# Folding the squared tiles of three norm entrances on VectorE, and moving the decay product behind the output gate, in a two-layer fp32 trunk

## The chip, the cores and the metric

The kernel runs on one core of one Trainium2 chip, in one launch. The metric is the device time in microseconds, from the first to the last instruction with what lies around them; of several runs the median is given. Five engines run their own instruction streams in program order and wait for one another by semaphores: TensorE (PE, its weight loads listed apart as PEld), VectorE (DVE), ScalarE (ACT), GpSimd (POOL) and SyncE (SP), which issues most of the DMAs.

## The reference

A trunk of two layers on x (1, 1024, 1024), all in fp32. Each layer is a token mixer and a dense SwiGLU channel mixer, each behind an RMS norm that is shifted and scaled by a conditioning vector. Layer 0's mixer is forgetting attention (FoX), layer 1's is gated linear attention (GLA).

```python
def rms_norm(x, g):
    xf = x.astype(jnp.float32)
    y = xf * lax.rsqrt(jnp.mean(xf * xf, axis=-1, keepdims=True) + EPS)
    return (y * g.astype(jnp.float32)).astype(x.dtype)

def gated_linear_attention(h, w_in, w_a2, b_a, g_o, w_out):
    proj = h @ w_in
    q, k, v, r, a_lr = jnp.split(proj, [...], axis=-1)
    log_alpha = jax.nn.log_sigmoid((a_lr @ w_a2 + b_a)) / GLA_TAU
    ...
    b = jnp.cumsum(log_alpha.reshape(B, N, CHUNK, GLA_HEADS, GLA_HK), axis=2)
    q_in = q * jnp.exp(b)
    k_in = k * jnp.exp(-b)
    A = tril(jnp.einsum('bnthk,bnshk->bnhts', q_in, k_in))
    k_dec = k * jnp.exp(b_last[:, :, None] - b)
    ...
    o = (o_intra + o_inter) * rsqrt(mean(o * o) + EPS) * g_o
    return (o * jax.nn.silu(r)) @ w_out

for i in range(DEPTH):
    h = modulate(rms_norm(x, norm1_g[i]), sh1, sc1)
    x = x + g1 * (forgetting_attention(h) if i % 2 == 0 else gated_linear_attention(h))
    h = modulate(rms_norm(x, norm2_g[i]), sh2, sc2)
    x = x + g2 * ((silu(h @ w_gate) * (h @ w_up)) @ ffn_w_out[i])
return rms_norm(x, final_g)
```

## The kernel before

Activations lie transposed: eight tiles of 128 features by 1024 tokens, worked on in two token halves of 512. Every fp32 product is three matmuls of high and low parts (lines 290, 291 and 292), so a product over 1024 features is 24 of them, of 512 columns each. FFN products go through sums and differences of sub-blocks (tiles `p_b`, with operands made from raw weights `xv_s` and `ex_s` by GpSimd at line 889 and after).

**Norm entrances.** The three entrances that matter here are the FFN of layer 0, the GLA mixer of layer 1 and the FFN of layer 1. `last_chunk` adds the last product's eight output tiles, one by one, into the residual x (line 1328). Behind each tile ScalarE squares it (line 764), and `SumSq.__call__` (line 771) adds squares pairwise, as a tree. For the second token half at these entrances (`late` = LATE1 = 7) the tree stops at four tiles, v0, v4, v6 and v7. Each of them is summed over its 128 features on TensorE, by four matmuls (`sp_b`, line 758: 128 tokens as weights, a column of ones as data), all accumulating in one PSUM bank. SUM_AT lets the first root's four go ahead, behind tile 5; the other twelve stand together later. In a profile such an fp32 matmul has two records, so sixteen matmuls show as 8 and 24. Then VectorE scales and adds epsilon (line 700), GpSimd takes the power −0.5 (line 701), and TensorE spreads the result over the partitions (`rb_b`, line 710), from where VectorE makes the normed input. The first token half is done earlier and is not touched.

**What sets the order.** Each engine's order is set ahead of time. Where the code asks for it with `issue_after`, an instruction is placed behind another in its engine's order. At the FFN entrances the work is the first products on the first token half, and the tuple GK says before which of the eight steps of the second plain tile the sums and the row broadcast stand. At the mixer `gv_first` plays that role: value products of one token tile each (`gv_b`, 24 matmuls of 272 columns), of which those for token tiles 0 to 3 need the first half only.

**The GLA mixer, head 0.** Behind the norm come the output gate's products `gr` (one per token half, 24 matmuls), the transposed low-rank gate inputs (`aps`, `a_body`), the decay product `z` (one matmul per half, line 1909), the key products `gk` and query products `gqp` (24 matmuls per half each). From z the decay is made: absolute value and minimum (1910, 1911), Exp and Ln (1918, 1919), a difference and two scans on VectorE (1923), Exp tiles (1933, 1934), which multiply gk out of PSUM (1948, 1949). `gr`, `z`, `gk` and `gqp` take turns in the three PSUM banks of the ring `pj`; a product can start when the readers of its bank are through. Weights come by DMA into a ring of three raw tiles (line 212), are cast to the high part on ScalarE (227) and subtracted to the low part in four pieces, three on GpSimd and one on VectorE (231). SP issues these loads in order, among those for the next layer vectors (`ad_s`, 427), which VectorE sums (488, 490).

Of the kernel before, what the change touches and what calls it, by code (L numbers as in the profile page):

```python
# [9 lines left out]
F32 = mybir.dt.float32  # L10
# [6 lines left out]
P = 128  # L17
# [3 lines left out]
HALF = 512  # L21
# [32 lines left out]
def trunk(ctx, tc, x, c, ada_w, ada_b, norm1_g, norm2_g, ffn_w_in, ffn_w_out,  # L54
# [54 lines left out]
    def psl(t, n=1):  # L109
        return slice(t * P, (t + n) * P)  # L110
# [576 lines left out]

    sp_ins, rb_ins, root_ins = [], [], {}
    LATE1 = 7
    SUM_AT = {5: 1, 7: 2}  # L690
    GK = (2, 6)
    SPM, RBM = (3, 4)

    def rms_cols(ss, nm, psr, n=4):

        ss.sums(psr, len(ss.roots))
        sp = ss.sp
        sp_ins.append(last_ins())
        rs = sm.tile([P, n], F32, tag="rs", name=f"rs{nm}")
        nc.vector.tensor_scalar(rs, sp, 1.0 / D, EPS, op0=ALU.mult, op1=ALU.add)  # L700
        nc.gpsimd.tensor_tensor(rs, rs, mhalf[:, 0:n], op=ALU.pow)
        root_ins.update(D=last_of("D"), G=last_of("G"))
        return rs
# [38 lines left out]
    class SumSq:  # L742


        def __init__(self, v, hf, late):
            w = slice(256 * (hf % 2), 256 * (hf % 2) + 256) if hf > 1 else slice(0, HALF)
            self.v = [v[i][:, w] for i in ((1, 3, 2, 5, 7, 6, 3, 4) if hf else range(8))]
            self.late = late
            self.n, self.sp, self.done = (2 if hf > 1 else 4), None, 0
            self.roots = {0: [self.v[0]], 8: [self.v[0]], 7: [self.v[0], self.v[4], self.v[6], self.v[7]]}[late]  # L750

        def sums(self, psr, upto):

            if self.sp is None:
                self.sp = psr([P, self.n], F32, "sp")
            for i in range(self.done, upto):
                for t in range(self.n):
                    nc.tensor.matmul(self.sp[:, t:t + 1], self.roots[i][:, psl(t)], ones, start=i == t == 0,
                                     stop=i == len(self.roots) - 1 and t == self.n - 1)
            self.done = upto  # L760

        def __call__(self, m, xk):
            v = self.v
            nc.scalar.activation(v[m], xk, AF.Square)
            if self.late == 0:
                if m:
                    nc.vector.tensor_add(v[0], v[0], v[m])
                return
            d = 1
            while m & d and m < self.late:  # L770
                (nc.gpsimd if d == 1 and m < 4 else nc.vector).tensor_add(v[m - 2 * d + 1], v[m - 2 * d + 1], v[m - d + 1])
                d *= 2

# [556 lines left out]
                if after is not None:  # L1330
                    after(m, hf)

    def last_chunk(k0, kc, hs, xs, l, j, nm, v, norm, mt=2, each=None, meanwhile=None, psr=None):


        behind = None
        for hf in (0, 2, 3) if each else (0, 1):
            sq = SumSq(v, hf, (0 if each else LATE1) if hf else 8)

            def after(m, h_, sq=sq):  # L1340
                sq(m, xs[m][:, hsl(h_)])
                if h_ == 1 and m in SUM_AT:
                    sq.sums(psr, SUM_AT[m])
                if each:
                    each(m, h_)
# [47 lines left out]
    def ffn(l, oh, xs, slots, nm, mid, norm_end, each=None):  # L1393
# [52 lines left out]
                split_t((b["B11"] + b["B21"])[k], ya[k], sh(k))  # L1446
            return gates

        last_chunk(4, 4, oh, xs, l, 2, nm, sv, norm, psr=psr)
        dump(f"xa{l}", xs)  # L1450
        sg = opr_["sg"]
        rb = rms_rows(ss1[0], f"{l}11", psr)
# [336 lines left out]
        sv = Views(slots["b"][0:4], 2, [HALF], f"se{l}").v  # L1789
        tmp = Views(slots["to"], 2, [HALF], f"te{l}")  # L1790
        last_chunk(NFH - 4, 4, hp, xs, l, 5, f"f{l}e", sv,
                   lambda hf, ss: norm_end(hf, ss, tmp), mt=1, each=each, meanwhile=meanwhile, psr=norm_banks)

    pin = None
    slots = ffn_slots(rest)
# [79 lines left out]
        nc.vector.tensor_sub(aT[32:48, cs], ps, aT[0:16, cs].bitcast(F32))  # L1875
        nc.scalar.copy(aT[64:80, cs], ps)

    def gv_first(t, wv, behind=None):

        if t % 2 == 0:  # L1880
            vt.append(vr([P, 2, 2, 256], FR, f"gvt0{t}"))
        ps = gvr([P, 272], F32, f"gv0{t}")
        with tc.issue_after(behind) if behind is not None else ExitStack():
            run(proj_tok(ps, wv, h1, t))
        nc.scalar.copy(aS[:, t], ps[:, 256:272])
        v = vt[-1]
        split(v[:, 0, t % 2], v[:, 1, t % 2], ps[:, 0:256])
# [49 lines left out]
    def head_front(h, b16, t2, ei, nmid):  # L1937
# [4 lines left out]
        for hf in range(2):  # L1942
            cs = hsl(hf)
            ps = pj([P, HALF], F32, f"gk{h}{hf}")
            run(proj(ps, wk, h1, hf))
            ada1(5.1)
            y = yv()
            nc.vector.tensor_mul(y, ps, ei[:, cs])
# [104 lines left out]
    def r_proj(h, gs, done):  # L2053
        wr_ = [None, None]
        for hf, dv in ((0, 0), (0, 1), (1, 0), (1, 1)) if h else ((0, 0), (1, 0), (0, 1), (1, 1)):
            if wr_[dv] is None:
                wr_[dv] = feed.next()
            ps = pj([P, HALF], F32, f"gr{h}{dv}{hf}")
            yield from proj(ps, wr_[dv], h1, hf)
            ada1(5.1)  # L2060
            nc.scalar.activation(gs[dv][:, hsl(hf)], ps, AF.Silu)
# [6 lines left out]
        w2_split()  # L2068
    split_after.update(marks)
    gvr = Ring(psp, list(pj.q) + list(opr.q))  # L2070
    aS = big.tile([P, 8, 16], F32, tag=kdr.q[0], name="aS")
    vt = []
    gv_first(0, wv)
    gv_first(1, wv)
    with tc.issue_after(sp_ins[-1]):
        gv_first(2, wv)
        gv_first(3, wv, rb_ins[-1])
    split_after.update((e, last_of(e)) for e in "AD")
    with behind_all():
        for f in rest_of_norm:  # L2080
# [9 lines left out]
        bt = gate_z(0, (0,))  # L2090
    for t in range(4, 8):
        gv_first(t, wv)
    while (0, 1) not in done:
        next(rg)
    a_body(1)
    b16, t2, ei, dec = gate_body(0, gate_z(0, (1,), bt))
    gtile = {}
    for h in range(4):
        dec, nmid = dec
# [102 lines left out]
```

## Time and profile before

| what | value |
|---|---|
| median of 3 runs | 2389.67 us (2388.23 to 2390.68) |
| profiled execution, its own time | 2393.87 us |
| its span, first to last instruction | 2392.2 us |
| mean granted TensorE clock | 0.991 |
| PE busy | 2362.3 us, 99% |
| DVE, ACT, POOL busy | 74%, 47%, 44% |
| longest waits of PE at the places of the change | 2.9 us (gqp), 1.3 us (gk) |

Busy shares are of the span. Rows of the timeline give start, duration, engine, line, operation, output and input tiles, shapes, a count, and in brackets how long the engine had been idle and what ended that. A row with x24 holds 24 records that followed each other, and its duration reaches from the first's start to the last's end.

### The profile page before, as it was taken

The numbers are of one execution on the slowest core, as the hardware profiler recorded it, in microseconds if no ns is written. First come the engines' busy times: TensorE is split into PE (matmuls) and PEld (weight loads), VectorE is DVE, ScalarE is ACT, GpSimd is POOL, SyncE is SP. The second block draws the span as 40 slices with busy tenths as digits, with TensorE's granted clock in tenths as the row PEclk, the third lists the DMA queues.
The fourth block names the chain that finished last, engine by engine and source line by source line (L and its number), as shares of the span: only waits on it lengthen the run. The fifth ranks groups of instructions, "written<-read, shape, count | busy, mean of one in ns | idle before, by whom it ended". The sixth has DMA issues, their size and how long they took to land.

```text
span 2392.2 us, 35827 instructions
## 1 busy us (share of the span) xinstructions
PE 2362.3 (99%) x12312; PEld 2012.5 (84%) x12312; DVE 1770.5 (74%) x2985; ACT 1128.8 (47%) x2178; POOL 1046.5 (44%) x976
## 2 busy tenths in 40 slices
PE   8999999999999999999999999999999999999998
PEld 6988888888888888888888798898888888888888
DVE  6577787886698788875798566655687877765787
ACT  6656565675443333345325555453443333345326
POOL 1334444533445566643264321212345666643262
PEclk8999999999999999999999999999999999999999
DMA  8423333342435545457655233334424544457664
GB/s 259 142 80 113 104 119 93 119 133 89 150 109 174 178 165 168 166 203 258 228 188 166 82 105 90 99 112 132 150 91 154 179 148 161 154 180 255 230 205 147
DMA packets 336366, 363.47 MB, mean 152 GB/s; under 512 B 24924, under 2 KB 278008, under 8 KB 336184
## 3 DMA queue, kind: packets, MB, share of 16 engines
q1 hardware_dynamic: 336184, 361.18, 46.3%
q8 instruction: 97, 1.59, 0.3%
q14 instruction: 85, 0.70, 0.1%
HBM read 268.22 MB, written 92.86 MB: 151 GB/s over the span
## 4 chain that ended last, share of the span: by engine, by line
PE 82%; DVE 8%; DMA 4%; ACT 2%; issue 2%; POOL 1%; SPq 1%; DVEq 0%; POOLq 0%; ACTq 0%
PE p_b L290 15%; PE p_b L292 15%; PE p_b L291 15%; PE o_b L1224 2%; PE t_b L1210 2%; PE qk_b L290 1%; PE qk_b L291 1%; PE qk_b L292 1%; PE gr_b L290 1%; PE gr_b L291 1%; PE vps_b L292 1%; PE vps_b L290 1%; PE vps_b L291 1%; PE gr_b L292 1%; PE s_b L1178 1%
## 5 line engine op out<-in xcount | busy, mean ns | idle before, releaser
L175 DVE TENSOR_TENSOR o_s<-xv_s,o_s 128x512 fp32r<-128x512 f32 (+1 forms) x376 | 326.7, 874 | 67.7 <-ACT o_s L174 67.3
L174 ACT CAST o_s<-xv_s 128x512 fp32r<-128x512 f32 (+1 forms) x376 | 216.4, 587 | 304.3 <-PE p_b L292 244.5
L291 PE MATMUL p_b<-B,o_s 128*128 128x512 f32 x608 | 237.8, 391 | 0.0
L292 PE MATMUL p_b<-B,o_s 128*128 128x512 f32 x608 | 237.2, 391 | 0.0
L290 PE MATMUL p_b<-B,o_s 128*128 128x512 f32 x608 | 236.0, 391 | 0.0
L889 POOL TENSOR_TENSOR ex_s<-xv_s,xv_s 128x512 f32<-128x512 f32 (+1 forms) x64 | 88.5, 1382 | 286.7 <-DMA xv_s<-in_ffn_w_in_dram 113.6
L1190 POOL TENSOR_SCALAR lp_s<-lp_s,st 128x128 f32<-128x128 f32 (+7 forms) x128 | 97.9, 769 | 249.5 <-DVE st L1189 235.5
L290 PE MATMUL p_b<-T,o_s 128*128 128x512 f32 x480 | 186.7, 389 | 0.0
L291 PE MATMUL p_b<-T,o_s 128*128 128x512 f32 x480 | 186.7, 389 | 0.0
L292 PE MATMUL p_b<-T,o_s 128*128 128x512 f32 x480 | 181.2, 389 | 0.0
L292 PEld LDWEIGHTS p_b<-B,o_s 128*128 128x128 f32 x608 | 114.7, 189 | 24.0
L290 PEld LDWEIGHTS p_b<-B,o_s 128*128 128x128 f32 x608 | 114.7, 189 | 23.9
L291 PEld LDWEIGHTS p_b<-B,o_s 128*128 128x128 f32 x608 | 114.7, 189 | 23.7
L1188 ACT ACTIVATE lp_s<-lp_s,st 128x128 f32<-128x128 f32 (+7 forms) x128 | 99.3, 776 | 62.3 <-DVE st L1184 61.2
L891 POOL TENSOR_TENSOR xv_s<-ex_s,xv_s 128x512 f32<-128x512 f32 (+1 forms) x64 | 87.3, 1365 | 63.1 <-DVE o_s L175 60.8
L174 ACT CAST pt_s<-t_b 128x512 fp32r<-128x512 f32 (+1 forms) x160 | 79.8, 547 | 71.9 <-PE t_b L1210 71.3
L231 POOL TENSOR_TENSOR w_l_s<-w__s,w_h_s 128x256 fp32r<-128x256 f32 x90 | 69.6, 802 | 94.2 <-ACT w_h_s L227 61.8
L175 DVE TENSOR_TENSOR pt_s<-t_b,pt_s 128x512 fp32r<-128x512 f32 (+1 forms) x160 | 96.3, 630 | 15.9 <-ACT pt_s L174 15.4
L1572 DVE TENSOR_TENSOR ex_s<-ex_s,p_b 128x512 f32<-128x512 f32 x140 | 93.6, 681 | 18.6 <-PE p_b L292 18.5
L290 PEld LDWEIGHTS p_b<-T,o_s 128*128 128x128 f32 x480 | 90.1, 188 | 18.8
L291 PEld LDWEIGHTS p_b<-T,o_s 128*128 128x128 f32 x480 | 90.1, 188 | 18.7
L292 PEld LDWEIGHTS p_b<-T,o_s 128*128 128x128 f32 x480 | 90.1, 188 | 18.6
(1967 smaller groups left out, 7408.3 us busy)
## 6 DMA issues: line engine op xcount, KB each, us to landing
xv_s<-in_ffn_w_in_dram SPq DMA_DIRECT2D x176, 256.0 KB, 3.3
hid_B<-x SPq DMA_DIRECT2D x70, 512.0 KB, 2.8
ad_s<-in_ada_w_dram SPq DMA_DIRECT2D x384, 64.0 KB, 2.4
hid_T<-x SPq DMA_DIRECT2D x36, 512.0 KB, 2.8
xv_s<-in_ffn_w_out_dram SPq DMA_DIRECT2D x96, 192.0 KB, 5.1
ada_s<-in_ada_w_dram SPq DMA_DIRECT2D x96, 128.0 KB, 2.8
xv_s<-in_ffn_w_out_dram SPq DMA_DIRECT2D x40, 256.0 KB, 2.8
T2o<-hid_T SPq DMA_DIRECT2D x18, 512.0 KB, 9.7
```

The lines of the kernel that those rows point to most:

```text
L174: nc.scalar.copy(hi, src)
L175: nc.vector.tensor_sub(lo, src, hi.bitcast(F32))
L231: (nc.gpsimd if i < 3 else nc.vector).tensor_sub(lo[:, cs], rw[:, cs], hi[:, cs].bitcast(F32))
L290: nc.tensor.matmul(ps, ah, bh, start=start, stop=False)
L291: nc.tensor.matmul(ps, ah, bl, start=False, stop=False)
L292: nc.tensor.matmul(ps, al, bh, start=False, stop=stop)
L889: nc.gpsimd.tensor_add(s1, a21, a22)
L891: nc.gpsimd.tensor_sub(a11, s1, a11)
L1188: nc.scalar.activation(lp, lp, AF.Exp, bias=mcur, scale=-1.0, accum_out=st[:, qi, 2:3])
L1190: nc.gpsimd.tensor_scalar(lp, lp, st[:, qi, 3:4], 1.0, op0=ALU.mult, op1=ALU.mult)
L1210: nc.tensor.transpose(tp[:, i, :], lps[qi][:, psl(2 * b + jj)], ident)
L1572: nc.vector.tensor_add(d, d if src is None else dest(G, src), ps)
```

## The change

Three things are changed. First, at the three entrances VectorE folds all eight squared tiles of the second token half into v0, in the order of their coming, and TensorE sums v0 alone, with four matmuls; the early part is gone. Second, the sums and the row broadcast stand one step later at the FFN entrances (GK from 2 and 6 to 3 and 7), and at the mixer within `gv_first(3)`. Third, in GLA head 0 the first `gr` product takes the bank of `atr`, the ring `pj` is turned by one, and the order on TensorE is set by hand: two steps of the second `gr`, the gate inputs' transposes, the rest of `gr`, z of the second half, and only then `gk`.

```diff
     LATE1 = 7
-    SUM_AT = {5: 1, 7: 2}
-    GK = (2, 6)
+    GK = (3, 7)
...
-        ss.sums(psr, len(ss.roots))
+        ss.sums(psr)
...
-            self.n, self.sp, self.done = (2 if hf > 1 else 4), None, 0
-            self.roots = {0: [self.v[0]], 8: [self.v[0]], 7: [self.v[0], self.v[4], self.v[6], self.v[7]]}[late]
-
-        def sums(self, psr, upto):
-
-            if self.sp is None:
-                self.sp = psr([P, self.n], F32, "sp")
-            for i in range(self.done, upto):
-                for t in range(self.n):
-                    nc.tensor.matmul(self.sp[:, t:t + 1], self.roots[i][:, psl(t)], ones, start=i == t == 0,
-                                     stop=i == len(self.roots) - 1 and t == self.n - 1)
-            self.done = upto
+            self.n = 2 if hf > 1 else 4
+            self.root = self.v[0]
+
+        def sums(self, psr):
+
+            self.sp = psr([P, self.n], F32, "sp")
+            for t in range(self.n):
+                nc.tensor.matmul(self.sp[:, t:t + 1], self.root[:, psl(t)], ones, start=t == 0, stop=t == self.n - 1)
...
+            if m > 4 and self.late == LATE1:
+                if m == 5:
+                    nc.vector.tensor_add(v[4], v[4], v[5])
+                    nc.vector.tensor_add(v[0], v[0], v[4])
+                else:
+                    nc.vector.tensor_add(v[0], v[0], v[m])
+                return
             d = 1
-            while m & d and m < self.late:
+            while m & d:
...
                 sq(m, xs[m][:, hsl(h_)])
-                if h_ == 1 and m in SUM_AT:
-                    sq.sums(psr, SUM_AT[m])
...
-    def gv_first(t, wv, behind=None):
+    def gv_first(t, wv, after=()):
...
-        with tc.issue_after(behind) if behind is not None else ExitStack():
-            run(proj_tok(ps, wv, h1, t))
+        g = proj_tok(ps, wv, h1, t)
+        for k in range(8):
+            with ExitStack() as es:
+                for k_, ins in after:
+                    if k >= k_:
+                        es.enter_context(tc.issue_after(ins))
+                next(g)
...
             ps = pj([P, HALF], F32, f"gk{h}{hf}")
-            run(proj(ps, wk, h1, hf))
+            with ExitStack() if h else tc.issue_after(z_last):
+                run(proj(ps, wk, h1, hf))
...
-            ps = pj([P, HALF], F32, f"gr{h}{dv}{hf}")
+            ps = (pj if h or hf or dv else atr)([P, HALF], F32, f"gr{h}{dv}{hf}")
...
     gvr = Ring(psp, list(pj.q) + list(opr.q))
+    pj.q.rotate(1)
...
-    with tc.issue_after(sp_ins[-1]):
-        gv_first(2, wv)
-        gv_first(3, wv, rb_ins[-1])
+    gv_first(2, wv)
+    gv_first(3, wv, ((0, sp_ins[-1]), (4, rb_ins[-1])))
...
-    while (0, 1) not in done:
+    for _ in range(2):
         next(rg)
-    a_body(1)
-    b16, t2, ei, dec = gate_body(0, gate_z(0, (1,), bt))
+    with tc.issue_after(last_of("P")):
+        a_body(1)
+    with tc.issue_after(last_of("P")):
+        while (0, 1) not in done:
+            next(rg)
+    with tc.issue_after(last_of("P")):
+        gate_z(0, (1,), bt)
+    z_last = last_of("P")
+    with tc.issue_after(last_of("A")):
+        b16, t2, ei, dec = gate_body(0, bt)
```

How this moves instructions, at three places. Each block lists consecutive rows of one engine's order (line, operation, output and inputs).

TensorE at the entrance of layer 0's FFN, before:

```order
L290 MATMUL p_b_1_7634<-B_7088,o_s_2_7433 128x512
L291 MATMUL p_b_1_7634<-B_7088,o_s_2_7433 128x512
L292 MATMUL p_b_1_7634<-B_7088,o_s_2_7433 128x512
L758 MATMUL sp_b_3_7428<-ones,ss_s_7080 128x1 x4
L758 MATMUL sp_b_3_7428<-ones,ss_s_7078 128x1 x4
L758 MATMUL sp_b_3_7428<-ones,ss_s_7079 128x1 x4
L290 MATMUL p_b_2_7664<-B_7083,o_s_3_7635 128x512
```

and with the change:

```order
L290 MATMUL p_b_1_7625<-B_7088,o_s_2_7429 128x512
L291 MATMUL p_b_1_7625<-B_7088,o_s_2_7429 128x512
L292 MATMUL p_b_1_7625<-B_7088,o_s_2_7429 128x512
L755 MATMUL sp_b_3_7464<-ones,ss_s_7077 128x1 x4
L290 MATMUL p_b_2_7655<-B_7084,o_s_3_7626 128x512
L291 MATMUL p_b_2_7655<-B_7084,o_s_3_7626 128x512
```

Twelve sum matmuls have become four, and the block stands behind one more step of the second tile (the operand that follows is B_7084, no longer B_7083); the four matmuls that stood 28 rows earlier are gone too.

VectorE at the same entrance, before:

```order
L1328 TENSOR_SCALAR x_6_6288<-fo1461p_b_15_7436,modc,x_6_6288 128x512
L1328 TENSOR_SCALAR x_7_6289<-fo1471p_b_16_7451,modc,x_7_6289 128x512
L771 TENSOR_TENSOR ss_s_7080<-ss_s_7080 128x512
L700 TENSOR_SCALAR rs_7478<-sp_b_3_7428 128x4
L1428 TENSOR_SCALAR yb_s_7502<-x_0_6282,amul,rb_b_4_7481 128x512
```

and with the change:

```order
L1330 TENSOR_SCALAR x_6_6288<-fo1461p_b_15_7432,modc,x_6_6288 128x512
L1330 TENSOR_SCALAR x_7_6289<-fo1471p_b_16_7448,modc,x_7_6289 128x512
L766 TENSOR_TENSOR ss_s_7080<-ss_s_7080 128x512
L767 TENSOR_TENSOR ss_s_7077<-ss_s_7077,ss_s_7080 128x512
L769 TENSOR_TENSOR ss_s_7077<-ss_s_7077,ss_s_7078 128x512
L769 TENSOR_TENSOR ss_s_7077<-ss_s_7077,ss_s_7079 128x512
L699 TENSOR_SCALAR rs_7469<-sp_b_3_7464 128x4
```

Three adds of 128x512 stand between the last one of before and the reader of the sums; each writes and reads the same tile.

TensorE in GLA head 0 around z of the second token half, before:

```order
L290 MATMUL gk_b_5_13378<-h1h_12669,w_h_s_85_12976 128x512
L291 MATMUL gk_b_5_13378<-h1l_12670,w_h_s_85_12976 128x512
L292 MATMUL gk_b_5_13378<-h1h_12669,w_l_s_86_12977 128x512
L290 MATMUL gr_b_3_13293<-h1h_12655,w_h_s_83_12966 128x512
...
L292 MATMUL gr_b_3_13293<-h1h_12669,w_l_s_84_12967 128x512
L1909 MATMUL z_b_4_13335<-aT,w2t 128x512
L290 MATMUL gk_b_6_13422<-h1h_12655,w_h_s_85_12976 128x512
```

and with the change:

```order
L292 MATMUL gv_b_8_13247<-wv_6h_s_81_12938,h1l_12659 128x272
L290 MATMUL gv_b_8_13247<-wv_6h_s_81_12938,h1h_12660 128x272
L291 MATMUL gv_b_8_13247<-wv_6l_s_82_12939,h1h_12660 128x272
L292 MATMUL gv_b_8_13247<-wv_6h_s_81_12938,h1l_12661 128x272
L290 MATMUL gr_b_2_13275<-h1h_12646,w_h_s_83_12948 128x512
...
L292 MATMUL gr_b_2_13275<-h1h_12660,w_l_s_84_12949 128x512
L1914 MATMUL z_b_3_13317<-aT,w2t 128x512
L290 MATMUL gk_b_4_13360<-h1h_12646,w_h_s_85_12958 128x512
```

The first gk half (24 matmuls) has moved from ahead of the second gr to behind z; both gk halves now follow z.

On the other engines: at the mixer VectorE's two memsets of `ad_s` come among the fold's adds; ScalarE's cast of the weight `wv_4` moves from between Ln and the next Exp to behind the first cast of `kih`; SP issues three more loads of `ad_s` ahead of the raw weight that gk uses.

More of the change, by code (lines that the diff above doesn't have):

```diff
@@ L1331, in out_chunk, with last_chunk @@
                     after(m, hf)
-    def last_chunk(k0, kc, hs, xs, l, j, nm, v, norm, mt=2, each=None, meanwhile=None, psr=None):
+    def last_chunk(k0, kc, hs, xs, l, j, nm, v, norm, mt=2, each=None, meanwhile=None):
         behind = None
@@ L1447, in norm @@
             return gates
-        last_chunk(4, 4, oh, xs, l, 2, nm, sv, norm, psr=psr)
+        last_chunk(4, 4, oh, xs, l, 2, nm, sv, norm)
         dump(f"xa{l}", xs)
@@ L1791, in ffn @@
         last_chunk(NFH - 4, 4, hp, xs, l, 5, f"f{l}e", sv,
-                   lambda hf, ss: norm_end(hf, ss, tmp), mt=1, each=each, meanwhile=meanwhile, psr=norm_banks)
+                   lambda hf, ss: norm_end(hf, ss, tmp), mt=1, each=each, meanwhile=meanwhile)
     pin = None
```

## The prediction

> **What bounds the kernel now.** I read the page's head, then TensorE's waits, and then the timeline at the three places that the change touches, with the granted clock of short stretches beside them.
>
> ```profile
> span 2392.2 us, 35827 instructions
> PE 2362.3 (99%) x12312; PEld 2012.5 (84%) x12312; DVE 1770.5 (74%) x2985; ACT 1128.8 (47%) x2178; POOL 1046.5 (44%) x976
> ```
>
> TensorE is busy 99% of the span, in program order. So an instruction taken from PE is worth what it occupies there, a wait of PE is worth its length, and a stretch at half clock what it lengthens. Everything else counts only when PE waits for it. The profiled execution took 2393.87 us (1.7 beyond its span), the three timed runs 2389.67 in the median; I sum against the span and take the 4.2 us off at the end.
>
> The first entrance (FFN of layer 0), from three looks at the timeline (start, us, engine, line):
>
> ```profile
> 648.68 0.95 PE L758 MATMUL sp_b<-ones,ss_s 128*128 128x1 f32 x8
> ...
> 653.45 0.68 DVE L771 TENSOR_TENSOR ss_s<-ss_s 128x512 f32<-128x512 f32 x1
> 653.55 1.73 POOL L889 TENSOR_TENSOR ex_s<-xv_s,xv_s 128x512 f32<-128x512 f32 x1 [14.13 <-DMA xv_s<-in_ffn_w_in_dram]
> 655.35 1.28 POOL L890 TENSOR_TENSOR xv_s<-xv_s 128x512 f32<-128x512 f32 x1
> 655.53 0.39 PE L291 MATMUL p_b<-B,o_s 128*128 128x512 f32 x1
> 655.75 0.39 PE L292 MATMUL p_b<-B,o_s 128*128 128x512 f32 x1
> 655.98 2.73 PE L758 MATMUL sp_b<-ones,ss_s 128*128 128x1 f32 x24
> 658.58 0.49 PE L290 MATMUL p_b<-B,o_s 128*128 128x512 f32 x1
> 658.75 0.16 DVE L700 TENSOR_SCALAR rs<-sp_b 128x4 f32<-128x4 f32 x1 [4.63 <-PE sp_b L758]
> 658.99 1.02 POOL L701 TENSOR_TENSOR rs<-rs,mhalf 128x4 f32<-128x4 f32 x1 [2.36 <-DVE rs L700]
> ...
> 661.44 1.05 PE L710 MATMUL rb_b<-ident,rs 128*128 128x128 f32 x8
> ```
>
> The reader is to see that 32 narrow records (16 matmuls) stand between the wide ones, eight early and 24 together, and that the 24 hold PE from 655.98 to 658.58. VectorE is idle from 654.13 to 658.75: that is where the added adds go. GpSimd works there on SBUF tiles of its own.
>
> The second FFN entrance has the same rows, and then something more:
>
> ```profile
> 1733.89 3.04 PE L758 MATMUL sp_b<-ones,ss_s 128*128 128x1 f32 x24
> 1742.05 1.50 PE L710 MATMUL rb_b<-ident,rs 128*128 128x128 f32 x8
> ...
> 1736.80:1742.00 5.20, 5.20 (x13) 4.09 (x14) 0.16 (x1) 0.00 (x0) 1.02 (x1) 0.50 0.00 0
> ```
>
> The last row is a stretch from the table of windows (length, then busy time of PE, of its weight loads, of VectorE, ScalarE and GpSimd, the granted clock, DMA share, GB/s): clock 0.50. From the 24 records to rb it is 8.16 us here and 5.46 at the first entrance, and rb is 0.45 longer: 3.15 us lost to the half clock. At the first entrance there was none.
>
> **Part 1, the sums.** Taking away 12 of 16 sum matmuls removes 24 of 32 records. The wide matmuls follow each other at 0.23 us (655.53, 655.75). The block of 24 costs 2.60, the eight early ones about 0.81, and each block 0.09 at the next matmul: 3.59 in all. Eight remain, at 0.90. **Saved 2.69 us at each entrance**, if PE does not wait.
>
> VectorE gets three more adds, behind the one at 653.45 and chained on v0. Alone, one is 0.68 long and a chained one starts 0.73 behind:
>
> ```profile
> 1275.25 0.69 DVE L771 TENSOR_TENSOR se_s<-se_s 128x512 f32<-128x512 f32 x1
> 1275.98 0.69 DVE L771 TENSOR_TENSOR se_s<-se_s,se_s 128x512 f32<-128x512 f32 x1
> ```
>
> Four adds from 653.45 end at 656.33. PE comes to the sums earlier than before, because the early eight are gone (0.90) and three more wide matmuls go first (0.68): at 655.71. It would stand 0.7, net gain 2.0. But GpSimd is at work beside the chain, and these rows show what an add of two SBUF tiles meets then:
>
> ```profile
> 622.61 1.81 DVE L771 TENSOR_TENSOR ss_s<-ss_s 128x512 f32<-128x512 f32 x1 [0.58 <-ACT ss_s L764]
> 622.59 2.99 POOL L771 TENSOR_TENSOR ss_s<-ss_s 128x512 f32<-128x512 f32 x2
> 629.85 2.41 DVE L771 TENSOR_TENSOR ss_s<-ss_s,ss_s 128x512 f32<-128x512 f32 x2
> 628.68 3.03 POOL L231 TENSOR_TENSOR wo_768l_s<-wo_s,wo_768h_s 128x256 fp32r<-128x256 f32 x3
> ```
>
> An add of 0.68 took 1.81 beside GpSimd adds, and two took 2.41 instead of 1.36; the two GpSimd adds took 1.5 each where L890 alone took 1.28. The L889 above, 0.45 longer than L890, started beside the one VectorE add. I read this as the two engines taking turns. Then, by the rows: add 1 to 654.13, L889 to 655.28, add 2 to 655.9, L890 to 657.1, add 3 to 657.8, add 4 to 658.4 or 658.5. PE stands 2.8 from 655.71 and comes out at 658.57 with 0.90 of sums ahead of it: **0.2 us later than before, not 2.0 earlier**. I take this value, since both GpSimd rows stand in the very gap; the other, 2.0 earlier, is the other bound. At the second FFN entrance the rows stand the same to 0.1 us, so the same 0.2.
>
> Moving sums and row broadcast by one tile step costs no instruction. rb comes 12 wide matmuls behind the sums (2.7 us), while L700, the power on GpSimd (about 1.0) and the hand-overs take about 1.5: covered, with 1.2 to spare; without that cover 0.3.
>
> Now the clock. An idle stretch of PE is followed by half clock at some places:
>
> ```profile
> 1344.20 0.39 PE L1909 MATMUL z_b<-aT,w2t 128*128 128x512 f32 x1
> 1345.91 0.50 PE L290 MATMUL gk_b<-h1h,w_h_s 128*128 128x512 f32 x1 [1.31 <-ACT gs_s L2061]
> 1356.69 0.39 PE L292 MATMUL gqp_b<-h1h,w_l_s 128*128 128x512 f32 x1
> 1359.96 0.50 PE L290 MATMUL gqp_b<-h1h,w_h_s 128*128 128x512 f32 x1 [2.88 <-DVE t_s L1949]
> 1367.16 0.38 PE L1975 MATMUL kdt_b<-ident,t_s 128*128 128x128 f32 x2
> ```
>
> The wait of 2.88 is: 24 matmuls then take 7.20 us (1359.96 to 1367.16) instead of 5.44, so 1.76 lost. The wait of 1.3 is not. The new wait of 2.8 with 0.9 of narrow sums behind it is like the first. So at each FFN entrance I add a stretch between 0 (as in layer 0 before) and 3.15 (as in layer 1 before), and take 1.8, the row nearest in kind. Layer 0: 0.2 + 1.8 = +2.0. Layer 1, where the old 3.15 goes: 0.2 + 1.8 − 3.15 = −1.2. **Both together +0.8 us**; bounds −7.1 (no turns, no half clock: −2.0 twice and −3.15) and +3.5.
>
> The Trainium skill, page "TensorE: Matmul & The Clock Gate", section Part 1, says that the clock halves after an idle window of some 3.4 us, free-running, and comes back after a busy one. The 1.76 lost over 3.8 us of half clock agree in the size; that a wait of 2.88 was enough does not agree with it. Taken strictly, a wait of 2.8 would cost no clock; that is a rival below.
>
> **Part 2, the mixer's entrance.** Its rows:
>
> ```profile
> 1297.16 0.29 PE L291 MATMUL gv_b<-wv_0l_s,h1h 128*128 128x272 f32 x1
> 1297.29 0.95 PE L758 MATMUL sp_b<-ones,se_s 128*128 128x1 f32 x8
> 1299.43 0.28 PE L290 MATMUL gv_b<-wv_0h_s,h1h 128*128 128x272 f32 x1
> 1299.81 2.84 PE L758 MATMUL sp_b<-ones,se_s 128*128 128x1 f32 x24
> ...
> 1299.68 0.74 DVE L1328 SCALAR_TENSOR_TENSOR x<-f0e11871p_b,modc,x 128x512 f32<-128x512 f32 x1
> 1301.04 0.48 DVE L1847 MEMSET ad_s<- 128x512 f32 x1 [0.62 <-PE sp_b L758]
> ...
> 1302.50:1306.10 3.60, 3.60 (x18) 3.60 (x18) 1.51 (x4) 2.00 (x4) 3.17 (x5) 0.53 0.36 105
> ```
>
> Saved again 2.69, plus an idle 0.25 ahead of the 24 (the next 272-column matmul would have been due at 1299.56), plus a half-clock stretch of 18 records in 3.60 us, which at the 0.126 of a full-speed step (1297.16 to 1297.29) are 2.27: 1.33. The sums now stand behind 54 gv matmuls, at about 1303.1 by that step. VectorE's last residual update ends at 1300.4; two adds, a memset of 0.48 and the last add bring the root to about 1302.8, and GpSimd, whose next instruction is the power behind L700, is idle there. No wait, 0.3 to spare: −4.3 us. rb follows 15 steps later (1.9 us) against the same 1.5.
>
> **Part 3, decay product behind the output gate.** Before, z of the second token half stands behind 24 gk matmuls and 24 gr matmuls; now gk comes behind z. Nothing is added on PE; the chain z, exp, log, scan, exp starts 24 matmuls (5.4 us) earlier relative to gk and gqp. Its rows:
>
> ```profile
> 1344.22 1.14 ACT L227 CAST wv_0h_s<-wv_s 128x512 fp32r<-128x512 f32 x2 [4.29 <-PE gr_b L291]
> 1352.47 3.27 DVE L1923 TENSOR_TENSOR_SCAN b_s<-ad_s,t_s 128x512 f32<-128x512 f32 x2
> 1352.19 4.07 POOL L231 TENSOR_TENSOR wv_4l_s<-wv_s,wv_4h_s 128x256 fp32r<-128x256 f32 x3 [4.98 <-ACT wv_4h_s L227]
> 1359.22 0.68 DVE L1949 TENSOR_TENSOR t_s<-gk_b,t_s 128x512 f32<-128x512 f32 x1
> ...
> 1332.75 0.37 SPq L212 DMA_DIRECT2D wv_s<-in_gla_w_in_dram  x1
> ...
> SPq L212 <- DVE w_l_s L231: 21.7, 1, 21.7
> ```
>
> The four products turn over three PSUM banks. The second gqp half needs the bank of the first gk half, read last by L1949, which ends 15.7 after z (1344.20 to 1359.90). Before it was wanted 12.7 after z; now 72 matmuls stand between, 16.6 after z. The second gk half needs the bank of gr, whose silu ended 1.7 after z, and is wanted 5.7 after. So both waits go, with 0.9 to spare at the tighter. It may be 2 to spare, as the cast of wv_4 moves behind and no longer puts GpSimd beside the scans. Gains: 1.48 (1344.20 + 0.23 to 1345.91), 3.04 (1356.69 + 0.23 to 1359.96) and the 1.76: −6.3. Moved on the queues: three loads for ada on SP ahead of one weight load; SP then sat waiting 21.7 us before (for VectorE's w_l), which covers them; without it some 2 us. The lo cast of wv_4 now runs beside VectorE's kil and gq splits, and the attention product after kdt has some 1 us of slack: I give 0.8 back, bounds 0 and 2.
>
> Sum: +0.8 − 4.3 − 6.3 + 0.8 = **−9.0**; span 2383.2, profiled execution 2384.9, median of timed runs 2380.7, say **2381**.
>
> **Rivals.** (a) The engines do not take turns at the fold, or L889 arrives earlier: FFN −7.1 instead of +0.8, 2373. For it: no row shows three such adds in this gap. Against it: 622.61 and 629.85.
>
> (b) They do, but no half clock follows: FFN 0.4 − 3.15 = −2.8, 2377. For it: layer 0 ran on at full clock behind 24 narrow records; against it: three of four such stretches did not. (The skill's 3.4 us window, read strictly, is this case.)
>
> (c) The mixer's gain is given back in part: the weight load of wv_0, issued at 1332.75 and landing some 4 to 5 later, used to have 6 us in hand; z now comes near 1334 and the load moves only by what its slot's last split moves, about 3. ScalarE takes its cast ahead of silu and of z's readers, so each microsecond of that load beyond the slack of 1 to 2 delays the second gqp half, and 1.76 of half clock comes with it. With the chain 4 late: 2 to 3 + 1.8, 2385 to 2387.
>
> (d) Slower: one mechanism, that same load. It goes out when the last split of the weight three loads ahead of it frees the slot (the wait of 21.7). ScalarE's cast for that split now stands behind the evacuation of one more gv tile. If the slot frees at 1338 or later instead of near 1330, the load lands at 1342 or later, the chain is 9 or more late, and PE pays all of that but the slack, with the half clock behind it: at 9 late 7.5 + 1.8, the whole gain; at 12 late 2393. So it decides from 9 us on. For it: ScalarE's order around these casts is rewritten. Against it: SP waits there for nothing else, so only one cast and its splits (4.07 for three at the worst) stand ahead.
>
> (e) The reordering does nothing for gk and gqp, because another reader holds the banks: −2.7, 2387. Against it: the releasers in brackets are L2061 and L1949, readers of just those banks.
>
> **How the numbers follow.** Forecast 0.38, (a) 0.17, (b) 0.13, (c) and (e) together 0.2, (d) 0.12. The range takes in (a) less 2, and on the other side (c), (e) and the beginning of (d): 2371 to 2391; the forecast's own is 2378 to 2385. A measurement tells some 0.2% (4.8 us) from no change: faster is below 2384.9. The forecast's case counts there with nearly all its weight, so do (a) and (b): faster 0.68; (c), (e) and part of (d) are the same, 0.21; slower 0.11.
>
> **What would show it.** In the changed profile: 8 sum records in one block at each entrance; at the FFN ones VectorE's last fold ending near 658.5 (turns) or 656.3 (none), GpSimd's L889 and L890 drawn apart, and PE idle 2.8 or 0.7 before the sums; the granted clock right behind them, 0.50 or 1.00; at the mixer no idle before the sums and no stretch at 0.5; gk and gqp without a wait, kdt about 10 us earlier. It is wrong if PE waits at gqp still, or if a new wait stands at at_b or behind wv_0.

## The result, and the profile after

The changed kernel takes 2384.86 us (median of 22 runs, 2382.06 to 2390.44), the kernel before 2390.39 in the same series (22 runs): ratio 0.9979, 95% interval 0.9973 to 0.9985. It is faster by 5.5 us in the medians. The forecast was 2381 with a range of 2371 to 2391, its own case 2378 to 2385.

The page of the changed kernel shows 2388.7 us of span against 2392.2. The profiled execution took 2390.42 us, more than all but one of the other runs, so it is not a typical one:

```profile
span 2388.7 us, 35698 instructions
PE 2357.6 (99%) x12240; PEld 2007.4 (84%) x12240; DVE 1782.2 (75%) x2994; ACT 1130.1 (47%) x2178; POOL 1041.1 (44%) x976
```

PE has 72 records fewer, the 3 times 24 of the sums. Where the time went is read best from landmarks that both programs have. These are rows of TensorE's timeline, first of the kernel before (the last residual product ahead of layer 0's FFN, the first of that FFN's output products, the last ahead of the mixer, the first kdt of head 0 and of head 1):

```profile
648.00 0.39 PE L292 MATMUL fo1471p_b<-ohh,wo_768l_s 128*128 128x512 f32 x1
...
1250.78 0.47 PE L290 MATMUL f0e01800p_b<-hh,oo_s 128*128 128x512 f32 x1 [0.33 <-issue]
...
1296.05 0.39 PE L292 MATMUL f0e11871p_b<-hh,oo_s 128*128 128x512 f32 x1
...
1367.16 0.60 PE L1975 MATMUL kdt_b<-ident,t_s 128*128 128x128 f32 x4
...
1438.09 0.60 PE L1975 MATMUL kdt_b<-ident,t_s 128*128 128x128 f32 x4
```

and the same of the changed kernel:

```profile
651.40 0.39 PE L292 MATMUL fo1471p_b<-ohh,wo_768l_s 128*128 128x512 f32 x1
...
1256.42 0.47 PE L290 MATMUL f0e01800p_b<-hh,oo_s 128*128 128x512 f32 x1 [0.31 <-ACT oo_s L922]
...
1301.72 0.39 PE L292 MATMUL f0e11871p_b<-hh,oo_s 128*128 128x512 f32 x1
...
1361.97 0.60 PE L1981 MATMUL kdt_b<-ident,t_s 128*128 128x128 f32 x4
...
1434.69 0.60 PE L1981 MATMUL kdt_b<-ident,t_s 128*128 128x128 f32 x4
```

The distances between them, less those of the first profile of the kernel before, make this table (us; "again" is a second profile of the same program, of which more below; the last column is from the last residual product ahead of layer 1's FFN to the first of its output products):

| kernel | FFN of layer 0 | mixer entrance to kdt of head 0 | to kdt of head 1 | FFN of layer 1 |
|---|---|---|---|---|
| before | 0 (602.78) | 0 (71.11) | 0 (70.93) | 0 (605.01) |
| before, again | +2.83 | −1.70 | +0.64 | −2.71 |
| changed | +2.24 | −10.86 | +1.79 | −0.10 |
| changed, again | +3.75 | −10.97 | +1.65 | −2.13 |
| gate only | −0.74 | −6.55 | +0.99 | −0.29 |
| fold only | +1.48 | −2.20 | +0.08 | +0.71 |
| GpSimd's sums moved | −1.07 | −10.96 | +1.67 | −4.91 |
| fold at the mixer only | +0.46 | −10.83 | +1.65 | −3.58 |
| ad_s sums later | +4.00 | −10.96 | +1.70 | −3.03 |
| both moves | −1.79 | −10.96 | +1.70 | −4.70 |
| FFN sums 2 steps later | −0.10 | −10.97 | +1.67 | −2.38 |
| moved, 1 step later | −1.59 | −10.85 | +2.08 | −3.39 |
| both moves, ahl first | −1.56 | −10.96 | +0.22 | −3.80 |

The rest of the programs agrees to some 0.3 us a stretch, but for the start: the first profile of the changed kernel comes to layer 0's first output product of the mixer 3.22 us later than the first of before, its second 1.43 earlier. The change touches nothing there; that is why the spans differ by only 3.5 us.

So the mixer gained 10.9, of which 1.8 came back within head 0, and the first FFN lost. This is its entrance, in the timelines of VectorE, GpSimd and TensorE of the changed kernel:

```profile
656.71 0.67 DVE L766 TENSOR_TENSOR ss_s<-ss_s 128x512 f32<-128x512 f32 x1
657.41 1.67 DVE L767 TENSOR_TENSOR ss_s<-ss_s,ss_s 128x512 f32<-128x512 f32 x1
659.19 2.37 DVE L769 TENSOR_TENSOR ss_s<-ss_s,ss_s 128x512 f32<-128x512 f32 x2
...
656.89 1.64 POOL L891 TENSOR_TENSOR ex_s<-xv_s,xv_s 128x512 f32<-128x512 f32 x1 [14.22 <-DMA xv_s<-in_ffn_w_in_dram]
658.61 1.60 POOL L892 TENSOR_TENSOR xv_s<-xv_s 128x512 f32<-128x512 f32 x1
...
661.70 1.02 PE L755 MATMUL sp_b<-ones,ss_s 128*128 128x1 f32 x8 [2.43 <-DVE ss_s L769]
...
1733.01 1.83 PE L755 MATMUL sp_b<-ones,ss_s 128*128 128x1 f32 x8 [2.62 <-DVE ss_s L769]
```

The first add, already there before, is 0.67 long. The second, beside L891 on GpSimd, takes 1.67, and the last two, of which the first stands beside L892, 2.37 together. The fold ends 4.85 us behind its start, and TensorE stands 2.43 us before the sums (2.62 at layer 1, where the eight records then take 1.83 instead of 1.02: half clock, a granted TensorE clock of 0.50).

In head 0 the two old waits are gone. The list of TensorE's waits from 1340 to 1400 of the changed kernel (us in total, times, longest):

```profile
PE go_b L290 <- ACT ahl_s L174: 0.7, 1, 0.7
PE kv_b L290 <- DVE Sf L2007: 0.4, 1, 0.4
PE kdt_b L1981 <- DVE kdl_s L175: 0.3, 1, 0.3
```

Three small new ones, 1.4 us together, stand in their place, at kdt and behind it: they make up most of the 1.8 that came back.

### The profile page after: what moved, and what is told of

Read it like the earlier page. It is cut to its first block, busy times and chain, and to the rows that moved or that the text cites. A ratio compares the mean times of both kernels' runs of the same rounds, so it can differ in the third digit from the quotient of the medians.

```text
span 2388.7 us, 35698 instructions
## 1 busy us (share of the span) xinstructions
PE 2357.6 (99%) x12240; PEld 2007.4 (84%) x12240; DVE 1782.2 (75%) x2994; ACT 1130.1 (47%) x2178; POOL 1041.1 (44%) x976
## 4 chain that ended last, share of the span: by engine, by line
PE 83%; DVE 8%; DMA 3%; issue 2%; ACT 2%; POOL 1%; SPq 1%; DVEq 0%; POOLq 0%; ACTq 0%
PE p_b L292 15%; PE p_b L290 15%; PE p_b L291 15%; PE o_b L1226 2%; PE t_b L1212 2%; PE qk_b L290 2%; PE qk_b L291 2%; PE qk_b L292 2%; PE vps_b L292 1%; PE vps_b L290 1%; PE vps_b L291 1%; PE gr_b L290 1%; PE gr_b L291 1%; PE gr_b L292 1%; PE s_b L1180 1%
## 5 line engine op out<-in xcount | busy, mean ns | idle before, releaser
L891 POOL TENSOR_TENSOR ex_s<-xv_s,xv_s 128x512 f32<-128x512 f32 (+1 forms) x64 | 88.5, 1382 | 287.1 <-DMA xv_s<-in_ffn_w_in_dram 112.9
L903 POOL TENSOR_TENSOR xv_s<-xv_s,xv_s 128x512 f32<-128x512 f32 x40 | 54.1, 1353 | 120.2 <-issue 72.5
L290 PEld LDWEIGHTS p_b<-T,o_s 128*128 128x128 f32 x480 | 90.1, 188 | 18.8
L291 PEld LDWEIGHTS p_b<-T,o_s 128*128 128x128 f32 x480 | 90.1, 188 | 18.7
```

The costliest lines, as they stand in the source:

```text
L290: nc.tensor.matmul(ps, ah, bh, start=start, stop=False)
L291: nc.tensor.matmul(ps, ah, bl, start=False, stop=False)
L891: nc.gpsimd.tensor_add(s1, a21, a22)
L903: nc.gpsimd.tensor_sub(r[A12], r[A12], r[A11])
```

## The experiments

My theory after the result: each part pays or costs at its own place; at the FFN entrances VectorE and GpSimd take turns; what comes back in head 0 is a chain that became the next to be late. All ratios are against the kernel before, timed in the same series; its median differs between series (2390.83, 2390.11 and 2388.85), so kernels of different series are best compared by their ratios.

**Each part alone.** The gate's part alone is the kernel before with these lines:

```diff
+            with ExitStack() if h else tc.issue_after(z_last):
+                run(proj(ps, wk, h1, hf))
...
+            ps = (pj if h or hf or dv else atr)([P, HALF], F32, f"gr{h}{dv}{hf}")
...
+    pj.q.rotate(1)
...
+    with tc.issue_after(last_of("P")):
+        gate_z(0, (1,), bt)
+    z_last = last_of("P")
```

> Only the third part of the change (decay product behind the output gate); the sums at all three entrances stay as before. Theory (each part pays at its own place): both waits of TensorE at gk and gqp go, with the half clock behind the second, -6.4 us at the first kdt; some 1.5 to 2 come back by the end of head 0, as with the whole change: 4.5 us faster than before, 2385.5. Rival (the give-back belongs to the fold's earlier start, not to the gate's order): the whole 6.4 stays, 2383.6. Rival (the gate's part alone does nothing, the mixer's gain all came from the shorter sums): within 1 us of before.

Measured: 2383.08 against 2390.83, ratio 0.9975 (0.9964 to 0.9986). The two waits are gone, −6.55 at kdt as expected (6.4). Afterwards +0.99 comes back, less than the 1.5 to 2 expected, and the second profile of the kernel before has +0.64 there with the old order. The time is some 2 us better than expected, inside the interval.

The fold alone is the changed kernel with those lines undone.

> Only the fold and the later sums at the three entrances; head 0 of the mixer in its old order. Theory: mixer's entrance -4.4, FFN of layer 0 +2.7, FFN of layer 1 about 0, together 1.7 us faster than before, 2388; the two waits at gk and gqp stand in the profile as before. Rival (the fold loses at the FFN entrances more than a profiled execution shows): no faster than before.

Measured: 2392.56 against 2390.83, ratio 1.0005 (0.9996 to 1.0014): no gain, the rival's side. The waits of this kernel from 1300 to 1400:

```profile
PE gqp_b L290 <- DVE t_s L1954: 2.9, 1, 2.9
PE gk_b L290 <- ACT gs_s L2066: 1.3, 1, 1.3
PE aps_b L316 <- ACT aS L1890: 0.6, 1, 0.6
PE gv_b L292 <- DVE h1l L722: 0.4, 1, 0.4
PE go_b L292 <- DVE ahl_s L175: 0.3, 1, 0.3
```

The old waits stand unchanged, and the shorter sums only bring TensorE sooner to two others. Its records show where the 4.3 us that the mixer's entrance should give went. Without the first wait, TensorE would come to the first aps 4.2 us earlier than before. Then it waits there (0.56) and at gv (0.36), and half clock follows: the 24 matmuls of the first gr take 7.13 us instead of 5.46. At the second gk half 0.6 us of the gain are left. The −2.20 at kdt is more only because the wait at gqp was not followed by half clock in this execution, as it was not in the second profile of the kernel before (−1.70). With the new order the shorter sums do pay: the changed kernel reaches kdt 4.31 us earlier than the gate's part alone. The FFN entrances lose in this profile, 1.48 and 0.71.

**Where the fold is worth it.** The changed kernel, but with the four roots, the early sums and GK (2, 6) at the FFN entrances:

```diff
-    GK = (3, 7)
+    SUM_AT = {5: 1, 7: 2}
+    FOLD = {2: False, 5: True}
+    GK = (2, 6)
...
-            if m > 4 and self.late == LATE1:
+            if m > 4 and self.fold:
```

> The fold at the mixer's entrance alone, with the third part; the two FFN entrances keep their four roots, the early sums and their old place. Theory (the FFN entrances together lose 2.6 us by the change): 2.6 us below the changed kernel, 2382, with the mixer as in the changed kernel. Rival (the FFN entrances gain or lose nothing): 2385. If layer 1's entrance keeps its half clock as before it costs 3.2 there.

Measured: 2379.88, ratio 0.9953 (0.9939 to 0.9967), the mixer as in the changed kernel (−10.83). Against the changed kernel (0.9979), not folding at the FFN entrances is worth 0.0026 of ratio, some 6 us, and 5.0 by the medians, more than the 2.6 expected; the intervals do not overlap.

**Why the fold is late at the FFN entrances.** The changed kernel, with GpSimd's two sums given to VectorE behind the fold, in both layers:

```diff
+                if m == 7:
+                    fold_ins.append(last_of("D"))
...
-        nc.gpsimd.tensor_add(s1, a21, a22)
-        nc.gpsimd.tensor_sub(a21, a11, a21)
+        E = nc.vector if gr == GROUPS[2] else nc.gpsimd
+        with tc.issue_after(fold_ins[-1]) if gr == GROUPS[2] and fold_ins else ExitStack():
+            E.tensor_add(s1, a21, a22)
+            E.tensor_sub(a21, a11, a21)
```

> The whole change, and at the two FFN entrances the two weight sums that GpSimd did beside the fold are done by VectorE behind the fold's last add. Theory (VectorE and GpSimd take turns, which holds the fold up): the four adds take 2.9 us in a row instead of 4.85, TensorE's wait ahead of the sums falls from 2.4-2.6 to about 0.5, no half clock follows; each entrance 2 to 3 us shorter, together 4 to 5.5 us below the changed kernel: 2380. Rival (three more chained adds are late whatever GpSimd does): the wait stays over 2, 2385. Rival (the two sums are needed early, and VectorE has no room for them): a new wait at the first products that use them, above 2385.

Measured: 2378.51, ratio 0.9948 (0.9936 to 0.9961). The entrance of layer 0 in this kernel's timelines of VectorE and TensorE, and the sums of layer 1:

```profile
651.86 0.68 DVE L767 TENSOR_TENSOR ss_s<-ss_s 128x512 f32<-128x512 f32 x1
652.58 0.69 DVE L768 TENSOR_TENSOR ss_s<-ss_s,ss_s 128x512 f32<-128x512 f32 x1
653.38 1.49 DVE L770 TENSOR_TENSOR ss_s<-ss_s,ss_s 128x512 f32<-128x512 f32 x2
654.78 0.69 DVE L896 TENSOR_TENSOR ex_s<-xv_s,xv_s 128x512 f32<-128x512 f32 x1
655.50 0.69 DVE L897 TENSOR_TENSOR xv_s<-xv_s 128x512 f32<-128x512 f32 x1
...
655.01 1.02 PE L756 MATMUL sp_b<-ones,ss_s 128*128 128x1 f32 x8 [0.53 <-DVE ss_s L770]
...
1722.84 1.02 PE L756 MATMUL sp_b<-ones,ss_s 128*128 128x1 f32 x8 [0.78 <-DVE ss_s L770]
```

The same four adds in the same chain now take 3.01 (651.86 to 654.87) instead of 4.85, and TensorE waits 0.53 and 0.78, with no half clock at either FFN entrance. What had made the chain late was GpSimd's two sums beside it, not its length. The Trainium skill, page "GPSIMD Engine Reference", section Key points, says that GpSimd shares its SBUF interfaces with VectorE and contends with VectorE instructions that have two SBUF inputs: these rows agree, and give the size, 1.84 us on the chain for two GpSimd sums.

Whether folding there, with the sums moved, beats not folding there is not settled by the times: 2378.51 and 2379.88 in one series, with overlapping intervals. In the table it does, by 2.9 in that pair of profiles.

**Waiting less instead.** The changed kernel with GK (5, 8): the sums two steps later, GpSimd as it was.

```diff
-    GK = (3, 7)
+    GK = (5, 8)
```

> The whole change, with the sums at the two FFN entrances two steps (six wide matmuls, 1.36 us) later and the row broadcast in front of the third tile; GpSimd keeps its two weight sums beside the fold. Theory (TensorE waits only because it comes to the sums before the fold is through): the wait of 2.4 to 2.6 falls to 1.1 to 1.3, a wait that at gk was not followed by half clock, so 1.4 us at each entrance and about 1 to 3 of half clock: 3 to 5 below the changed kernel, 2380 to 2382. Rival (a later row broadcast makes the normed input late by 0.7): a new wait in the tiles that follow, 2383 or more.

Measured: 2381.44, ratio 0.9962 (0.995 to 0.9975). The waits of this kernel at layer 0 (rows of TensorE's timeline):

```profile
657.68 1.02 PE L755 MATMUL sp_b<-ones,ss_s 128*128 128x1 f32 x8 [1.05 <-DVE ss_s L769]
...
668.39 0.50 PE L291 MATMUL p_b<-B,o_s 128*128 128x512 f32 x1 [0.47 <-DVE B L1436]
```

As the theory had it the wait falls to 1.05 (1.30 in layer 1), and no half clock stands behind it; the rival is right too, in part: the normed input B is late, 0.47. The same step by 0.68 on top of the moved sums, GK (4, 8):

> The two GpSimd sums on VectorE behind the fold, and sums and row broadcast one step (0.68 us) later. Theory: the rest of TensorE's wait, 0.5 to 0.8 at each entrance, goes: 1.2 us below that kernel, 2377.3. Rival (the normed input becomes late): no gain or a loss.

Measured: 2378.54, ratio 0.9949 (0.9936 to 0.9963), no gain. No wait is left at the sums, but one of 0.45 for B stands in its place.

**What came back in head 0.** First guess: a vector sum for the next layer that waits for its DMA on VectorE. In the changed kernel this stood ahead of the second gqp half's products (VectorE's timeline):

```profile
1366.63 0.49 DVE L490 SCALAR_TENSOR_TENSOR ad_s<-ad_s,c,ad_s 128x256 f32<-128x256 f32 x1 [1.27 <-issue]
1367.03 0.68 DVE L1969 SCALAR_TENSOR_TENSOR gy_s<-gqp_b,ei_s 128x512 f32<-128x512 f32 x1
```

```diff
             run(proj(ps, wq, h1, hf))
-            ada1(5.1)
+            if h:
+                ada1(5.1)
...
+        if not h:
+            ada1(10.2)
```

> The whole change, and in head 0 the vector sums for the next layer (ad_s) that VectorE had between the two halves of gqp stand behind the second half's products. Theory (one of those sums waits there for its DMA with the products of the second gqp half queued behind it, 1.3 us idle and 4.5 us late for gy, and the attention products follow late): most of the 1.7 us that come back between the first kdt of head 0 and that of head 1 stay, 1 to 1.5 us below the changed kernel: 2383.5 to 2384. Rival (ScalarE, with Exp and Ln of head 1's gate ahead of the cast for go, sets that stretch): no change, 1.7 us come back all the same. Rival (the sums only wait elsewhere, ahead of the masked copy of the attention product): slower there by up to 1.

Measured: 2385.34 against 2390.11, ratio 0.9977 (0.9967 to 0.9986): the same as the changed kernel. The products came forward and +1.70 came back all the same. This theory fell. On top of the moved sums:

> The kernel with the two GpSimd sums on VectorE behind the fold, and the ad_s sums of head 0 behind the second gqp half. Theory: both gains add, 1 to 1.5 below the former, 2377 to 2377.5. Rival: no gain on it, 2378.5.

Measured: 2377.28, ratio 0.9946 (0.9934 to 0.9959); 1.2 below 2378.51, which the intervals cannot tell from nothing, and +1.70 in head 0 again.

Second guess: the order on ScalarE. In the changed kernel the masked attention product's cast stood behind Exp and Ln of head 1's gate (ScalarE's timeline):

```profile
1382.85 1.28 ACT L1923 ACT_TABLE_LOAD   x1
1384.14 1.06 ACT L1923 ACTIVATE t_s<-t_s 128x1024 f32<-128x1024 f32 x1
1385.22 1.28 ACT L1924 ACT_TABLE_LOAD   x1
1386.52 1.06 ACT L1924 ACTIVATE t_s<-t_s 128x1024 f32<-128x1024 f32 x1
1387.48 0.60 ACT L174 CAST ahl_s<-atz_s 128x512 fp32r<-128x512 f32 x1
```

```diff
-        nc.scalar.activation(t2, t2, AF.Exp, scale=-1.0)
+        with tc.issue_after(ahl_ins[-1]) if h == 1 else ExitStack():
+            nc.scalar.activation(t2, t2, AF.Exp, scale=-1.0)
...
+            ahl_ins.append(last_of("A"))
```

> The fastest kernel so far (fold with GpSimd's two sums on VectorE behind it, ad_s sums late), and ScalarE's cast of the second masked attention product of head 0 (ahl) ahead of Exp and Ln of head 1's gate. Theory (what comes back in head 0 is TensorE waiting for casts that stand behind Exp and Ln and their table loads on ScalarE): of the waits of 0.9, 0.5 and 0.5 at go and kv at least one goes, the stretch from the first kdt of head 0 to that of head 1 gets 0.5 to 1 shorter, 2376.5. Rival (it is the chain of states through VectorE, which no order on ScalarE shortens): the waits stay, 2377.3, or the gate of head 1 comes later and costs as much.

Measured: 2376.87, ratio 0.9953 (0.9939 to 0.9966). ScalarE's timeline of this kernel, and all that its list of TensorE's waits has left from 1340 to 1400:

```profile
1372.30 0.62 ACT L174 CAST ahl_s<-atz_s 128x512 fp32r<-128x512 f32 x1
1372.94 1.28 ACT L1930 ACT_TABLE_LOAD   x1
...
PE go_b L291 <- DVE S_t L175: 0.4, 1, 0.4
```

The stretch to kdt of head 1 shrinks from +1.70 to +0.22: in the profile the mechanism is shown, for the kernel whose ad_s sums are late; this order on ScalarE was not tried without them. The times show no gain. The median is 0.4 below 2377.28, but in a series on another chip, where the kernel before is faster too; the ratio is 0.9953 against 0.9946, with overlapping intervals.

**How far one profile can be trusted.** The kernel before and the changed kernel were profiled once more.

> The kernel before, profiled once more. Theory (half clock at the FFN entrance of layer 1 depends on where the chip's clock window happens to lie, as layer 1's entrance showed none in the kernel that kept its old sums there): the 24 records there, or at layer 0, may go with or without half clock this time; the time from the last matmul of the residual products to the first of the last FFN product differs by up to 3 us from the first profile. Rival (it always follows at this place): 3.0 us for the 24 records and half clock behind them again.

> The changed kernel, profiled once more. Theory: the waits of 2.4 and 2.6 at the FFN entrances stand again to 0.1 us, the half clock behind them may fall otherwise by up to 3 us; the 3.3 us that the first profile lost in its first 70 us, where the change touches nothing, do not come again. Rival: all of it repeats.

Measured: 2391.51 and 2384.40, one run each. Two stretches of the second profile of the kernel before (the table of windows, granted clock before the last two columns):

```profile
658.00:662.00 4.00, 4.00 (x11) 3.09 (x10) 0.00 (x0) 0.00 (x0) 0.89 (x1) 0.50 0.00 0
...
1738.00:1742.00 4.00, 4.00 (x23) 3.40 (x23) 1.25 (x2) 0.47 (x1) 0.59 (x2) 1.00 0.00 0
```

and of the first one at the same places:

```profile
658.00:662.00 4.00, 4.00 (x25) 3.47 (x25) 0.16 (x1) 0.00 (x0) 1.02 (x1) 1.00 0.01 4
...
1738.00:1742.00 4.00, 4.00 (x10) 3.08 (x10) 0.00 (x0) 0.00 (x0) 0.22 (x1) 0.50 0.00 0
```

The same program has the half clock at layer 1 in one execution and at layer 0 in the other (+2.83 and −2.71 in the table), and at gqp only in the first (−1.70). In the changed kernel too it changed places: the waits stood again at 2.43 and 2.62, with 1.84 for the sums of layer 0 and 1.02 for layer 1. The 3.3 us of the start did not come again.

## Why the prediction was right, and where it was off

**Right: what bounds the kernel and the gate's part.** TensorE's program order carried everything. The gate's part was put at −6.3; alone it measures −6.55 at kdt. In part this is luck: 1.76 of it is the half clock behind the wait at gqp, which the second profile of the kernel before does not have, and against that profile it is −4.85. (The clock record of the first has 3.41 us at half clock there, where the working read 3.8.) Both waits went, the bank of the second gqp half had room, and rivals (c), (d) and (e) about the load of wv_0 and other readers did not occur.

**Right: the mixer's entrance, −4.3.** Together −10.9 at kdt against −10.6 forecast, and no wait at the sums; the changed kernel less the gate's part alone is −4.31. The half clock behind the 24 records, 1.33 of the forecast, stands in all three profiles with the old sums there (the kernel before twice, gate only). That in the old order most of this gain is lost again was not foreseen.

**Right: the turns.** The adds were forecast to end 5.0 behind the first one's start; they end 4.85 behind. TensorE's wait was put at 2.8 and is 2.43 and 2.62. The experiment that takes GpSimd away confirms the cause, not only the size. Rival (a) fell: 622.61 and 629.85 were the rows to believe.

**Mis-sized: the two FFN entrances, "both together +0.8".** The working took the old 3.15 of half clock at layer 1 as gone for certain, and charged 1.8 at each place for the new one. In four profiles with the old FFN entrances (before twice, gate only, fold at the mixer only) the two FFN stretches sum to 0, +0.12, −1.03 and −3.12, mean −1.0; in four with the fold beside GpSimd (changed twice, fold only, ad_s later) to +2.14, +1.62, +2.19 and +0.97, mean +1.7. So the term is +2.7 and not +0.8. The clock records split it. Three of the first four profiles have 6.83 us at half clock in these stretches and one has none; of the other four, two have 6.83 and two 10.24. Half of that is time lost: 2.6 us on average against 4.3, where the working had 3.15 against 3.6. The other +1.0 is at full clock, where it had +0.4. The half clock that I booked as a gain was one execution's lot; any of these stretches has it at times.

**Mis-sized: "I give 0.8 back".** It is 1.65 to 1.79 against 0 and 0.64 in the two profiles of before, so about 1.4. The cause that I gave, contended splits near the first attention product, was not the one: it is the cast behind Exp and Ln on ScalarE.

The sum with the measured terms: FFN +2.7; mixer −10.9 against a mean of −0.85 in the two profiles of before, −10.1; give-back +1.4; together −6.0. Timed: −5.5. The forecast's −9.0 was too large chiefly by the FFN term, and 2384.86 lies just inside its own 2378 to 2385.

By the medians, the FFN entrances cost 5.0 (2384.86 against 2379.88), and not 2.7. The two do not contradict each other: 2379.88 is the fold at the mixer only, the one profile of the four with no half clock at these entrances (−3.12), and the two profiles of the changed kernel, mean +1.9, lie 5.0 above it. Whether that kernel escapes the half clock by its timing or was lucky is open; its five runs lie within 1.6 us.

## What to carry to other kernels

An add moved to an idle engine is free only if nothing holds it up there: look which engine works on SBUF in that gap, and move that work behind the chain, which here took away the loss at two of three places (2378.5 instead of 2384.9; 2379.9 without the fold there). Stalls that are gone at one place come back where the next engine's order was made for the old timing; look for casts that stand behind a table load. And do not book half-clock stretches of one profile as gains: profile the same kernel twice first.

## What was not expected of the hardware

Waits of 2.4 to 2.9 us of TensorE were followed by half clock in some executions and not in others: the 2.62 of the changed kernel at layer 1 once with 1.83 for the eight sums, once with 1.02; the 2.88 at gqp with clock 0.50 in the first profile of before, with 1.00 in the second. The clock records of the thirteen profiles show what decides. From 70 us after the start to 30 us before the end, every stretch at half clock lasts 3.41 or 6.83 us, and within one execution all of them start on one grid of 3.41 us.

So each execution can be cut into windows along its own grid, and for each window the columns of the matmul records that start in it can be counted (128x512 is 512 columns; a window of wide matmuls has about 7700). At full clock, 23 windows had fewer than 3072 columns, and half clock followed every one. Nine had 3072 to 3280, and it followed three. 8613 had more, and it followed none. What the chip itself counts is not shown; this count tells the cases apart.

It explains the two profiles of before. These are windows of their grids at gqp, two of the first and three of the second, with the length, the busy time of PE, PEld, DVE, ACT and POOL, and then the granted clock:

```profile
1357.27:1360.68 3.41, 0.72 (x3) 0.64 (x4) 1.29 (x2) 3.41 (x14) 0.00 (x0) 1.00 0.55 154
1360.69:1364.10 3.41, 3.41 (x9) 2.63 (x9) 3.15 (x6) 3.41 (x11) 0.00 (x0) 0.50 0.00 0
...
1356.50:1359.91 3.41, 1.87 (x9) 1.21 (x7) 1.54 (x6) 2.30 (x9) 1.05 (x1) 1.00 0.12 29
1359.92:1363.33 3.41, 2.09 (x9) 1.75 (x10) 2.36 (x4) 3.41 (x12) 0.00 (x0) 1.00 0.41 124
1363.33:1366.74 3.41, 3.41 (x17) 2.82 (x16) 3.41 (x8) 3.41 (x10) 0.00 (x0) 1.00 0.00 0
```

The same wait fell almost whole into one window in the first and was split between two in the second. Narrow sums weigh next to nothing in the count, though TensorE is busy with them. At the mixer's entrance before, with hardly a wait:

```profile
1299.25:1302.66 3.41, 3.32 (x29) 3.10 (x28) 1.71 (x4) 2.84 (x7) 0.05 (x1) 1.00 0.89 348
1302.66:1306.07 3.41, 3.41 (x16) 3.41 (x17) 1.51 (x4) 1.84 (x4) 3.14 (x5) 0.50 0.33 96
```

The first of these windows has 840 columns. So a short wait is no safe one either: behind the 0.56 at aps in the fold-only kernel, in a window of 2416 columns, half clock came too.

The Trainium skill ("TensorE: Matmul & The Clock Gate", Part 1) has a free-running window of about 3.4 us, and half clock after an idle one. The grid agrees with the first; the second is too narrow for this case, where windows in which TensorE was busy for 0.72 to 3.41 us were enough.
